# A hybrid decoder layer on one core: decay rows in HBM by chunk, and a third slot for the gating tile

## The chip, the core and the metric

The kernel runs on one core of a Trainium2 chip. The core has five engines that run side by side, each through its own instructions in order: TensorE (PE, matrix products), VectorE (DVE), ScalarE (ACT), GpSimd (POOL), and SyncE (SP), which here only issues transfers. Transfers run on 16 DMA engines between HBM and the on-chip memory of 128 partitions. The metric is the device time of one execution in microseconds (us).

## What is computed

One layer of a decoder over 1024 tokens (and 16 learned ones ahead): a projection of the normed input feeds three branches (linear attention, sliding-window attention, and a state-space branch, SSD), which are gated, merged, projected and followed by an MLP. The change concerns SSD alone. Cut to that:

```
a_cs = jnp.cumsum(dtc * A, axis=2)                          # decay sums inside a chunk of 128 tokens
xdt = xc * dtc[..., None]
seg = a_cs[:, :, :, None] - a_cs[:, :, None, :]
Lmat = jnp.exp(jnp.where(causal[:, :, None, None], seg, -jnp.inf))
CB = jnp.einsum('bnlgd,bnsgd->bnlsg', Cc, Bc)
y_diag = jnp.einsum('bnlsgh,bnsghp->bnlghp', CB[..., None] * Lmat, xdt)
...
y_off = jnp.einsum('bnlgd,bnghpd->bnlghp', Cc, S_prev) * jnp.exp(a_cs)[..., None]
y = y_diag + y_off + D_skip.astype(f32).reshape(SSD_GROUPS, SSD_HPG)[:, :, None] * xc
y = y.reshape(bsz, L, SSD_DINNER) * jax.nn.silu(z.astype(f32))
y = y * lax.rsqrt(jnp.mean(y * y, axis=-1, keepdims=True) + EPS)    # per group of 512 channels
```

There are 32 heads of 64 channels, in four groups of eight heads, and eight chunks of 128 tokens.

## The kernel before

Everything runs in float32; large products are made of three passes over a high and a low part of each operand. A first phase holds the normed input on chip and makes all projections; a second does the branch projections, merging and the MLP.

Early in the first phase the cumulated decays of all 32 heads stand in the tile `stk`, one head per partition. L753 stores them to HBM as `acs_d`, 32 rows of 1024 tokens. Behind it on SP come `dec_d` (L754), its load `decb` (L758) and weight loads (`w_raw`, L160).

The function `ssd(g)` (L570) does one group. It makes the convolved inputs, then a loop over eight chunks `c` (L651), with two slots each for most tiles. A chunk goes like this:

- SP loads `ab` (L654): the chunk's 128 decays of each of the group's eight heads, the same for all 128 partitions (512 KB on chip), and `zt` (L656), the gate, 256 KB.
- VectorE subtracts each partition's own decay (L658, eight instructions), ScalarE takes Exp (L660), VectorE multiplies by C·B (L661) and makes xd (L663).
- TensorE multiplies `ab` by xd, head by head (L666), then makes the part from the state (L672) and the state's update (L683).
- VectorE sums y (L677, L676, L678) and the new state (L686); GpSimd prepares some terms (L674, L681, L685).
- y is multiplied by `zt` (L688), squared and summed by ScalarE, which writes over `zt` (L690), scaled (L86, L88, L692), transposed by TensorE (L644) and stored (`y_out`, L641).

A slot of `ab` is free when L666 of the chunk two before has read it. A slot of `zt` is free when L690 of its chunk has ended. In between, TensorE gets products of other stages as fillers: the gates (`fill`, stores from L224) and the next group's z (`zfill`, L199 to L201, stored to `zd` by L213); their weights come through L160, and L143 and L144 split them into high and low parts (three slots for `w_raw`). A scheduler sets the order of each engine's instructions when the kernel is built, from the priorities in the code; the chip keeps that order.

Of the kernel before, what the change touches and what calls it, by code (L numbers as in the profile page):

```python
# [8 lines left out]
F32 = mybir.dt.float32  # L9
# [7 lines left out]
P = 128  # L17
D = 1024
KD = D // P
SEQ = 1024  # L20
NM = 16
T = NM + SEQ
NT = SEQ // P
# [21 lines left out]
def hybrid_layer_kernel(ctx, tc, x, meta_tokens, norm_mix, w_in, b_gate, gla_w_gate_up, gla_b_gate_up,  # L45
# [3 lines left out]
    nc = tc.nc  # L49
# [10 lines left out]
    dram = ctx.enter_context(tc.tile_pool(name="dram", bufs=1, space=DRAM))  # L60
# [46 lines left out]
    ossd = [dram.tile([512, SEQ], F32, name=f"ossd{g}") for g in range(4)]  # L107
    gated = [dram.tile([P, SEQ], F32, name=f"gate{i}") for i in range(24)]
    zd = [dram.tile([SEQ, 512], F32, name=f"zd{i}") for i in range(4)]
    acs_d = dram.tile([32, SEQ], F32, name="acs_d")  # L110
    dec_d = dram.tile([32, NT], F32, name="dec_d")
    x2_d = dram.tile([SEQ, D], F32, name="x2_d")
    hid_d = {(q, n): dram.tile([256, 512], F32, name=f"hid{q}_{n}")
# [65 lines left out]
    with p1:  # L179
# [390 lines left out]
        def ssd(g):  # L570
            CH = 512
# [78 lines left out]
            with tc.high_priority(offset=HPE):  # L650
                for c in range(NT):  # L651
                    cs = slice(NM + c * P, NM + (c + 1) * P)
                    ab = ep.tile([P, 8, P], F32, tag="ab", name="ab", bufs=2)
                    nc.sync.dma_start(ab, acs_d[8 * g:8 * g + 8, c * P:(c + 1) * P].partition_broadcast(P))  # L654
                    zt = ep.tile([P, CH], F32, tag="zt", name="zt", bufs=2)
                    nc.sync.dma_start(zt, zd[g][c * P:(c + 1) * P, :])  # L656
                    for h in range(8):
                        nc.vector.tensor_scalar(ab[:, h, :], ab[:, h, :], tms[:, c, 32 + 8 * g + h:33 + 8 * g + h], 0.0,  # L658
                                                op0=sub, op1=amin)
                    nc.scalar.activation(ab, ab, AF.Exp)  # L660
                    nc.vector.tensor_tensor(ab, ab, up(cb[:, c, :], 1, [P, 8, P]), mult)  # L661
                    xd = ep.tile([P, CH], F32, tag="xd", name="xd", bufs=2)
                    nc.vector.tensor_tensor(r3(xd), r3(xT[:, c, :]), tcol(c, 0), mult)  # L663
                    psD = bank(bk, "y", 3)
                    for h in range(8):
                        mm = nc.tensor.matmul(psD[:, h * 64:(h + 1) * 64], lhsT=ab[:, h, :],  # L666
                                              rhs=xd[:, h * 64:(h + 1) * 64], start=True, stop=True)
                    if c:
                        with tc.issue_after(mm.ins):
                            y_out(c - 1, yn)  # L670
                    psY = bank(bk, "y", 3)
                    nc.tensor.matmul(psY, lhsT=CF[:, cs], rhs=S, start=True, stop=True)  # L672
                    y = ep.tile([P, CH], F32, tag="y", name="y", bufs=2)
                    nc.gpsimd.tensor_tensor(r3(y), r3(xT[:, c, :]), up(db[:, 8 * g:8 * g + 8], 2, s3), mult)  # L674
                    t2 = ep.tile([P, CH], F32, tag="t2", name="t2", bufs=1)
                    nc.vector.tensor_tensor(r3(t2), r3(psY), tcol(c, 2), mult)  # L676
                    nc.vector.tensor_tensor(y, y, psD, add)  # L677
                    nc.vector.tensor_tensor(y, y, t2, add)  # L678
                    if c < NT - 1:
                        xe = ep.tile([P, CH], F32, tag="xe", name="xe", bufs=2)  # L680
                        nc.gpsimd.tensor_tensor(r3(xe), r3(xT[:, c, :]), tcol(c, 3), mult)  # L681
                        psS = bank(bk, "y", 3)
                        nc.tensor.matmul(psS, lhsT=BT[:, c, :], rhs=xe, start=True, stop=True)  # L683
                        S2 = ep.tile([P, CH], F32, tag="S", name="S", bufs=2)
                        nc.gpsimd.tensor_tensor(r3(S2), r3(S), up(decb[:, 8 * g:8 * g + 8, c], 2, s3), mult)  # L685
                        nc.vector.tensor_tensor(S2, S2, psS, add)  # L686
                        S = S2
                    nc.vector.tensor_tensor(y, y, zt, mult)  # L688
                    ss = sm.tile([P, 1], F32, tag="ss", name="yss")
                    nc.scalar.activation(zt, y, AF.Square, accum_out=ss)  # L690
                    rs = rstd_of(ss, CH, "yrs")
                    nc.scalar.activation(y, y, AF.Copy, scale=rs)  # L692
                    yn = y
                y_out(NT - 1, yn)
# [4 lines left out]
        with tc.tile_pool(name="dtp", bufs=1, reuse_waits="tile") as dp, bank_pool("bdt") as bk:  # L699
            def loads(raw, i):  # L700
                rv = raw.rearrange("p (k c) -> p k c", k=KD // 2)
                ks = slice(i * (KD // 2), (i + 1) * (KD // 2))
                nc.gpsimd.memset(rv[:, :, 16:32], 0.0)
                nc.sync.dma_start(rv[:, :, 0:16], w_in_v[:, ks, GLR:GLR + 16])
                nc.sync.dma_start(rv[:, :, 32:64], w_in_v[:, ks, MDT:MDT + 32])
            w = w_split(loads, 64)
            dtb = dp.tile([64, 1], F32, name="dtb")
            nc.scalar.dma_start(dtb[32:64, :], ssd_dt_bias[0].unsqueeze(1))
            an = dp.tile([64, 1], F32, name="an")
            nc.scalar.dma_start(an[32:64, :], ssd_A_log[0].unsqueeze(1))  # L710
            r = slice(32, 64)
            nc.scalar.activation(an[r], an[r], AF.Exp)
            nc.vector.tensor_scalar(an[r], an[r], -1.0, None, op0=mult)
            e = dp.tile([64, T], F32, name="dte")
            dt = dp.tile([64, T], F32, name="dt")

            def ev(ps, c0, n):
                nc.scalar.copy(lrT[:, c0:c0 + n], ps[0:16])
                nc.scalar.activation(e[r, c0:c0 + n], ps[r], AF.Abs, bias=dtb[r])
                nc.vector.tensor_scalar(dt[r, c0:c0 + n], ps[r], dtb[r], 0.0, op0=add, op1=amax)  # L720
            fm(w, 0, 64, PIECES, ev)
            wv_ = dp.tile([64, T], F32, name="dtw")
            ln = dp.tile([64, T], F32, name="dtl")
            nc.scalar.activation(e[r], e[r], AF.Exp, scale=-1.0)
            nc.vector.tensor_scalar(wv_[r], e[r], 1.0, None, op0=add)
            nc.scalar.activation(ln[r], wv_[r], AF.Ln)
            nc.vector.tensor_tensor(dt[r], dt[r], ln[r], add)
            nc.vector.tensor_scalar(ln[r], wv_[r], -1.0, None, op0=add)
            nc.vector.tensor_tensor(e[r], e[r], ln[r], sub)
            nc.vector.reciprocal(wv_[r], wv_[r])  # L730
            nc.vector.tensor_tensor(e[r], e[r], wv_[r], mult)
            nc.vector.tensor_tensor(dt[r], dt[r], e[r], add)
            stk = dp.tile([P, T], F32, name="stk")
            nc.vector.tensor_scalar(ln[r], dt[r], an[r], None, op0=mult)
            rst = dp.tile([64, T], F32, name="rst")
            nc.gpsimd.memset(rst[r], 1.0)
            nc.gpsimd.memset(rst[r, 0:1], 0.0)
            nc.gpsimd.memset(rst[r, NM:].rearrange("p (c t) -> p c t", t=P)[:, :, 0:1], 0.0)
            nc.vector.tensor_tensor_scan(out=stk[r], data0=rst[r], data1=ln[r], initial=0.0, op0=mult, op1=add)
            nc.scalar.copy(stk[0:32], dt[r])  # L740
            nc.scalar.activation(stk[64:96], stk[r], AF.Exp)
            sr = stk[r, NM:].rearrange("p (c t) -> p c t", t=P)
            nc.vector.tensor_tensor(wv_[r, NM:].rearrange("p (c t) -> p c t", t=P),
                                    sr[:, :, P - 1:P].broadcast_to([32, NT, P]), sr, sub)
            nc.vector.tensor_scalar(wv_[r, 0:NM], stk[r, 0:NM], stk[r, NM - 1:NM], -1.0, op0=sub, op1=mult)
            nc.scalar.activation(wv_[r], wv_[r], AF.Exp)
            nc.vector.tensor_tensor(stk[96:128], dt[r], wv_[r], mult)
            for t in range(NT + 1):
                ps = bank(bk, "tr", 4)
                c0, n = (NM + t * P, P) if t < NT else (0, NM)  # L750
                nc.tensor.transpose(out=ps[:n, :P], in_=stk[:, c0:c0 + n], identity=ident)
                nc.vector.tensor_copy(tms[:n, t, :], ps[:n, :P])
            nc.sync.dma_start(acs_d, stk[r, NM:])  # L753
            nc.sync.dma_start(dec_d.unsqueeze(2), stk[64:96, NM:].rearrange("p (c t) -> p c t", t=P)[:, :, P - 1:P])  # L754
        zfill(1000)
        fill(FD)
# [23 lines left out]
    with ExitStack() as p2:  # L780
# [68 lines left out]
        for b in range(2):  # L849
            for k in range(KD):  # L850
                t = hl_tile()
# [293 lines left out]
        for i in range(2):  # L1145
            t = hl_tile().bitcast(F32)
# [71 lines left out]
        for q in range(NQ):  # L1218
# [28 lines left out]
            c = four()  # L1247
# [44 lines left out]
```

## Time and profile before

| | us |
|---|---|
| median of 3 runs (2694.1 to 2702.11) | 2696.54 |
| the profiled execution | 2697.15 |
| its span, first to last instruction | 2695.5 |
| TensorE busy | 2612.5 (97%) |
| VectorE busy | 1502.5 (56%) |
| ScalarE busy | 1096.4 (41%) |
| GpSimd busy | 513.9 (19%) |

The mean granted clock of TensorE over the span is 0.983 of full speed. The four chunk loops of SSD run at about 940 to 1035, 1122 to 1217, 1327 to 1415 and 1505 to 1590 us of the span; the stretches between them make the next group's inputs. In a row of the timeline the time in brackets is how long the engine had stood idle before, with what released it; a busy TensorE isn't TensorE at its peak, since matrix products overlap.

### The profile page before, as it was taken

How to read it: one execution, taken by the hardware profiler on the slowest of the kernel's cores; microseconds unless marked ns; L12 is line 12 of the kernel's file. 1: busy time of each engine (PE TensorE's matmuls, PEld its weight loads, DVE VectorE, ACT ScalarE, POOL GpSimd, SP SyncE). 2: the span in 40 equal slices, each digit the busy share in tenths (PEclk: the TensorE clock that was granted, in tenths of full speed). 3: DMA queues.
4: the chain of work that ended last, by engine and by line, in shares of the span. 5: the costliest groups of instructions: out<-in, count | busy, mean ns of one | idle time of the engine just before them, and what ended most of it. 6: DMA issues, size and time to landing. Idle time of an engine off the chain costs nothing.

```text
span 2695.5 us, 36835 instructions
## 1 busy us (share of the span) xinstructions
PE 2612.5 (97%) x14373; PEld 2245.8 (83%) x14373; DVE 1502.5 (56%) x2577; ACT 1096.4 (41%) x1930; POOL 513.9 (19%) x402
## 2 busy tenths in 40 slices
PE   8999999999999989989989999999999999999998
PEld 7998988888888979869879778888898888878887
DVE  5333323256664674563665664254437878777777
ACT  6423423246664454353364343233216222333334
POOL 1000000002221030130120210222200433353223
PEclk9999999999999989989999999999999999999999
DMA  4211112212223143252252365343234644574442
GB/s 143 64 46 49 48 48 62 80 50 72 68 65 100 48 109 95 59 121 87 57 137 65 84 213 172 102 157 102 87 132 145 202 158 149 188 273 142 150 149 79
DMA packets 253747, 293.54 MB, mean 109 GB/s; under 512 B 16014, under 2 KB 184260, under 8 KB 253572
## 3 DMA queue, kind: packets, MB, share of 16 engines
q1 hardware_dynamic: 199876, 223.48, 27.8%
q10 hardware_dynamic: 52736, 64.56, 6.8%
q0 software_dynamic: 960, 3.15, 0.4%
q8 instruction: 113, 1.85, 0.3%
q14 instruction: 62, 0.51, 0.1%
HBM read 213.93 MB, written 77.20 MB: 108 GB/s over the span
## 4 chain that ended last, share of the span: by engine, by line
PE 83%; DMA 8%; DVE 4%; ACT 3%; issue 2%; POOL 0%; SPq 0%; ACTq 0%; DVEq 0%; POOLq 0%
PE pp_ps L798 9%; PE acc_ps L171 9%; PE acc_ps L172 9%; PE acc_ps L173 8%; DMA ab<-acs_d 6%; PE pp_ps L801 4%; PE pp_ps L1204 4%; PE pp_ps L1205 4%; PE pp_ps L1202 3%; PE pp_ps L954 3%; PE pp_ps L957 3%; PE pp_ps L956 3%; PE acc_ps L199 3%; PE acc_ps L201 3%; PE acc_ps L200 3%
## 5 line engine op out<-in xcount | busy, mean ns | idle before, releaser
L171 PE MATMUL acc_ps<-hh,w_hi 128*128 128x512 f32 (+6 forms) x1320 | 473.0, 358 | 2.4 <-ACT rt L365 1.7
L172 PE MATMUL acc_ps<-hl,w_hi 128*128 128x512 f32 (+6 forms) x1320 | 473.5, 359 | 0.0
L173 PE MATMUL acc_ps<-hh,w_lo 128*128 128x512 f32 (+6 forms) x1320 | 472.4, 358 | 0.0
L199 PE MATMUL acc_ps<-w_hi,hh 128*128 128x256 f32 x1056 | 305.0, 289 | 4.2 <-ACT zst L212 4.1
L201 PE MATMUL acc_ps<-w_hi,hl 128*128 128x256 f32 x1056 | 307.0, 292 | 0.0
L200 PE MATMUL acc_ps<-w_lo,hh 128*128 128x256 f32 x1056 | 306.7, 291 | 0.0
L171 PEld LDWEIGHTS acc_ps<-hh,w_hi 128*128 128x128 f32 (+1 forms) x1320 | 247.5, 188 | 32.7 <-issue 3.7
L144 DVE TENSOR_TENSOR w_lo<-w_raw,w_hi 128x1024 fp32r<-128x1024 f32 (+1 forms) x124 | 156.9, 1267 | 204.4 <-ACT w_hi L143 201.1
L173 PEld LDWEIGHTS acc_ps<-hh,w_lo 128*128 128x128 f32 (+1 forms) x1320 | 247.7, 188 | 26.7 <-issue 2.7
L172 PEld LDWEIGHTS acc_ps<-hl,w_hi 128*128 128x128 f32 (+1 forms) x1320 | 247.4, 187 | 26.8 <-issue 2.4
L143 ACT CAST w_hi<-w_raw 128x1024 fp32r<-128x1024 f32 (+1 forms) x124 | 128.4, 1036 | 206.9 <-PE acc_ps L172 86.7
L199 PEld LDWEIGHTS acc_ps<-w_hi,hh 128*128 128x128 f32 x1056 | 198.7, 188 | 12.3 <-issue 5.9
L201 PEld LDWEIGHTS acc_ps<-w_hi,hl 128*128 128x128 f32 x1056 | 198.6, 188 | 11.7 <-issue 11.0
L200 PEld LDWEIGHTS acc_ps<-w_lo,hh 128*128 128x128 f32 x1056 | 198.6, 188 | 6.3 <-issue 4.9
L798 PE MATMUL pp_ps<-o,w_hi 128*128 128x512 f32 x512 | 201.5, 398 | 1.1 <-ACT gst L223 1.1
L801 PE MATMUL pp_ps<-o,w_hi 128*128 128x512 f32 x512 | 200.5, 392 | 0.0
L1204 PE MATMUL pp_ps<-w_lo,o 128*128 128x512 f32 x448 | 178.5, 399 | 3.7 <-DVE w_lo L1192 3.7
L1205 PE MATMUL pp_ps<-w_hi,o 128*128 128x512 f32 x448 | 178.2, 398 | 0.0
L1202 PE MATMUL pp_ps<-w_hi,o 128*128 128x512 f32 x448 | 176.1, 397 | 1.2 <-ACT w_hi L1191 1.2
L954 PE MATMUL pp_ps<-o,w_hi 128*128 128x512 f32 x448 | 176.1, 396 | 1.1 <-ACT o L165 0.8
L956 PE MATMUL pp_ps<-o,w_hi 128*128 128x512 f32 x448 | 177.1, 395 | 0.0
L957 PE MATMUL pp_ps<-o,w_lo 128*128 128x512 f32 x448 | 176.3, 395 | 0.0
(326 smaller groups left out, 5150.5 us busy)
## 6 DMA issues: line engine op xcount, KB each, us to landing
w_raw<-in_w_in_dram SPq DMA_DIRECT2D x80, 512.0 KB, 3.8
ab<-acs_d SPq DMA_DIRECT2D x32, 512.0 KB, 8.9
g<-gate SPq DMA_DIRECT2D x64, 256.0 KB, 3.6
w_raw<-in_w_mlp_in_dram SPq DMA_DIRECT2D x32, 512.0 KB, 3.6
hid_t<-mt ACTq DMA_DIRECT2D x64, 256.0 KB, 2.3
raw<-hid_t SPq DMA_DIRECT2D x32, 512.0 KB, 4.0
gate<-gst ACTq DMA_DIRECT2D x48, 256.0 KB, 2.5
hid_x<-hid ACTq DMA_DIRECT2D x48, 256.0 KB, 3.2
```

Source lines behind the costliest of these rows:

```text
L171: nc.tensor.matmul(ps, lhsT=lh, rhs=rh, start=(i == 0), stop=False)
L172: nc.tensor.matmul(ps, lhsT=lh, rhs=rl, start=False, stop=False)
L173: nc.tensor.matmul(ps, lhsT=ll, rhs=rh, start=False, stop=(i == n - 1))
L199: nc.tensor.matmul(o, lhsT=h_h, rhs=whi[:, k, off:off + width], start=(k == 0), stop=False)
L200: nc.tensor.matmul(o, lhsT=h_h, rhs=wlo[:, k, off:off + width], start=False, stop=False)
L201: nc.tensor.matmul(o, lhsT=h_l, rhs=whi[:, k, off:off + width], start=False, stop=(k == KD - 1))
L798: nc.tensor.matmul(ps[b], lhsT=lh, rhs=xs[b][:, 0, :], start=(st and k == 0), stop=(sp_ and k == n - 1))
L801: nc.tensor.matmul(ps[b], lhsT=lh, rhs=xs[b][:, 1, :], start=False, stop=False)
L956: nc.tensor.matmul(ps, lhsT=h[:, kk, :], rhs=x[:, 1, :], start=False, stop=False, skip_group_check=True)
L957: nc.tensor.matmul(ps, lhsT=l[:, kk, :], rhs=x[:, 0, :], start=False, stop=(last and kk == 3), skip_group_check=True)
L1204: nc.tensor.matmul(ps[t], lhsT=xh[:, ts], rhs=wl, start=False, stop=False, skip_group_check=True)
L1205: nc.tensor.matmul(ps[t], lhsT=xl[:, ts], rhs=wh, start=False, stop=(last and kk == 3), skip_group_check=True)
```

## The change

`acs_d` becomes four arrays, one for each group, with a chunk's eight heads side by side: 8 x 128 floats, 4 KB in one piece. The load of `ab` reads this piece once for each partition, where it read eight pieces of 512 B, 4 KB apart. The one store of 32 x 1024 becomes four, each from eight partitions. And `zt` gets a third slot.

```
-    acs_d = dram.tile([32, SEQ], F32, name="acs_d")
+    acs_d = [dram.tile([NT, 8, P], F32, name=f"acs_d{g}") for g in range(4)]
...
-                    nc.sync.dma_start(ab, acs_d[8 * g:8 * g + 8, c * P:(c + 1) * P].partition_broadcast(P))
-                    zt = ep.tile([P, CH], F32, tag="zt", name="zt", bufs=2)
+                    nc.sync.dma_start(ab.rearrange("p h t -> p (h t)"), acs_d[g][c].rearrange("h t -> (h t)").partition_broadcast(P))
+                    zt = ep.tile([P, CH], F32, tag="zt", name="zt", bufs=3)
...
-            nc.sync.dma_start(acs_d, stk[r, NM:])
+            for g in range(4):
+                nc.sync.dma_start(acs_d[g].rearrange("c h t -> h c t"),
+                                  stk[32 + 8 * g:40 + 8 * g, NM:].rearrange("h (c t) -> h c t", t=P))
```

The instructions of TensorE, VectorE, ScalarE and GpSimd stand in the same order as before (lines behind the store are two higher). Only SP's queue differs.

First place: SP at the start of the second group's chunk loop. `zd_125` is that group's gate, `acs_d_129` its decays; weights (`w_raw`) stand between. Before:

```order
L654 DMA ab<-acs_d 128x8x128
L656 DMA zt<-zd_125 128x512 x2
L160 DMA w_raw<-in_w_in_dram 128x4x128 x2
L160 DMA w_raw<-in_w_in_dram 128x4x256 x7
L654 DMA ab<-acs_d 128x8x128
L656 DMA zt<-zd_125 128x512
L654 DMA ab<-acs_d 128x8x128
L656 DMA zt<-zd_125 128x512
L654 DMA ab<-acs_d 128x8x128
L656 DMA zt<-zd_125 128x512
```

and now:

```order
L656 DMA zt<-zd_125 128x512
L654 DMA ab<-acs_d_129 128x1024
L656 DMA zt<-zd_125 128x512 x2
L160 DMA w_raw<-in_w_in_dram 128x4x128 x2
L160 DMA w_raw<-in_w_in_dram 128x4x256 x7
L654 DMA ab<-acs_d_129 128x1024
L656 DMA zt<-zd_125 128x512
L654 DMA ab<-acs_d_129 128x1024
L656 DMA zt<-zd_125 128x512
L654 DMA ab<-acs_d_129 128x1024
```

Ahead of the nine weight loads there are now three `zt` loads of the group instead of two; behind them `ab` and `zt` still take turns, with each `zt` that of one chunk later than before.

Second place: SP at the end of the second group's loop, where the third group's first loads begin (`zd_126`, `acs_d_130`). Before:

```order
L654 DMA ab<-acs_d 128x8x128
L160 DMA w_raw<-in_w_in_dram 128x4x256
L654 DMA ab<-acs_d 128x8x128
L656 DMA zt<-zd_125 128x512
L654 DMA ab<-acs_d 128x8x128
L656 DMA zt<-zd_125 128x512
L654 DMA ab<-acs_d 128x8x128
L160 DMA w_raw<-in_w_in_dram 128x4x256
L160 DMA w_raw<-in_w_in_dram 128x4x128 x2
L656 DMA zt<-zd_126 128x512 x2
```

and now:

```order
L654 DMA ab<-acs_d_129 128x1024
L160 DMA w_raw<-in_w_in_dram 128x4x256
L654 DMA ab<-acs_d_129 128x1024
L656 DMA zt<-zd_125 128x512
L654 DMA ab<-acs_d_130 128x1024 x2
L160 DMA w_raw<-in_w_in_dram 128x4x256
L160 DMA w_raw<-in_w_in_dram 128x4x128 x2
L656 DMA zt<-zd_126 128x512 x3
```

The last `zt` of the second group no longer stands between the third group's first two `ab` loads, and the third group loads three `zt` in a row.

## Rows read from the trace of the kernel before

**Rows 1.** Busy time in the four chunk loops, with granted clock

```profile
core 0: us, PE busy (x) PEld busy (x) DVE busy (x) ACT busy (x) POOL busy (x), PEclk, DMA share, GB/s
940.00:1035.00 95.00, 83.34 (x546) 71.19 (x545) 61.45 (x132) 51.75 (x73) 28.58 (x26) 0.89 0.50 125
1122.00:1217.00 95.00, 79.28 (x426) 63.57 (x424) 55.06 (x126) 41.53 (x60) 28.23 (x25) 0.86 0.46 109
...
1327.00:1415.00 88.00, 73.92 (x489) 62.37 (x488) 59.27 (x127) 50.78 (x71) 24.70 (x25) 0.94 0.51 123
1505.00:1590.00 85.00, 76.70 (x356) 59.03 (x354) 53.51 (x111) 28.92 (x48) 28.11 (x25) 0.90 0.40 110
```

**Rows 2.** The same view, 5 us of the second loop, behind an idle stretch

```profile
1152.00:1157.00 5.00, 5.00 (x19) 3.97 (x18) 2.10 (x3) 1.66 (x3) 1.37 (x1) 0.50 0.60 103
```

**Rows 3.** Line L654, who waited (us, times), and its landing

```profile
  DVE ab L658: 98.6, 27
...
DMA to landing us min/median/max: 7.5/8.9/10.2
```

**Rows 4.** SP's issues in the second loop, in order of time

```profile
1125.61 0.37 SPq L654 DMA_DIRECT2D ab<-acs_d  x1
1137.30 0.34 SPq L656 DMA_DIRECT2D zt<-zd  x1
1137.73 0.39 SPq L654 DMA_DIRECT2D ab<-acs_d  x1
```

**Rows 5.** ScalarE in the second loop, in order of time

```profile
1137.09 0.18 ACT L690 ACTIVATION_READ_ACCUMULATOR zt<-y 128x1 f32 x1
```

**Rows 6.** TensorE in the second loop, in order of time

```profile
1131.15 1.89 PE L666 MATMUL ps_y<-xd,ab 128*128 128x64 f32 x16
...
1150.33 0.69 PE L666 MATMUL ps_y<-xd,ab 128*128 128x64 f32 x2 [3.26 <-DVE y L677]
```

**Rows 7.** VectorE in the second loop, in order of time

```profile
1133.91 1.66 DVE L658 TENSOR_SCALAR ab<-ab,tms 128x128 f32<-128x128 f32 x8 [4.89 <-DMA ab<-acs_d]
...
1145.56 1.66 DVE L658 TENSOR_SCALAR ab<-ab,tms 128x128 f32<-128x128 f32 x8 [4.58 <-DMA ab<-acs_d]
...
1150.19 0.68 DVE L663 TENSOR_TENSOR xd<-xT,tms 128x512 f32<-128x512 f32 x1
```

**Rows 8.** Stretches as in rows 1, one us with the `ab` load in flight

```profile
1129.00:1130.00 1.00, 1.00 (x6) 0.77 (x6) 0.03 (x1) 0.00 (x0) 0.94 (x1) 1.00 0.39 87
```

**Rows 9.** The load of final_norm: its issue, and two us of its flight

```profile
L1236 SPq DMA_DIRECT2D o<-in_final_norm_dram x1: 340/340/340, 2620.0 to 2620.0; - x1
...
2621.00:2622.00 1.00, 1.00 (x6) 0.82 (x5) 1.00 (x1) 1.00 (x2) 1.00 (x1) 1.00 0.88 340
2622.00:2623.00 1.00, 1.00 (x6) 0.82 (x5) 1.00 (x1) 0.53 (x1) 0.09 (x1) 1.00 0.47 172
```

**Rows 10.** SP's issues behind the second loop, in order of time

```profile
1230.19 1.02 SPq L656 DMA_DIRECT2D zt<-zd  x2
1246.44 75.78 SPq L160 DMA_DIRECT2D w_raw<-in_w_in_dram  x9
```

**Rows 11.** SP's issues around the store of the decays

```profile
73.64 0.34 SPq L753 DMA_DIRECT2D acs_d<-stk  x1
```

**Rows 12.** Stretches as in rows 1, 10 us behind that store

```profile
80.00:90.00 10.00, 10.00 (x81) 8.80 (x80) 3.62 (x7) 3.69 (x7) 0.00 (x0) 1.00 0.59 143
```

**Rows 13.** VectorE in the third loop, in order of time

```profile
1364.78 0.29 DVE L658 TENSOR_SCALAR ab<-ab,tms 128x128 f32<-128x128 f32 x1 [0.92 <-DMA ab<-acs_d]
...
1374.55 2.41 DVE L658 TENSOR_SCALAR ab<-ab,tms 128x128 f32<-128x128 f32 x8 [0.18 <-DMA ab<-acs_d]
```

**Rows 14.** TensorE in the third loop, in order of time

```profile
1373.77 2.46 PE L666 MATMUL ps_y<-xd,ab 128*128 128x64 f32 x16 [1.76 <-DVE ms L86]
```

**Rows 15.** Issues of transfers: line, tile, count, KB each, us to landing

```profile
w_raw<-in_w_in_dram SPq DMA_DIRECT2D x36, 256.0 KB, 3.5
```

## The prediction

> **What bounds the kernel now.** I read the stages first (busy time of each engine in chosen stretches), then who waits for the `ab` load, then the queue of SP and the order of time on VectorE, ScalarE and TensorE inside one loop. Over the whole span TensorE is busy 2612.5 of 2695.5 us, so only 83 us of its idle time can be won, plus what a lowered clock costs. Both sit mostly in four short stretches: the chunk loops of the four SSD groups [rows 1]. There TensorE is busy 83.34 of 95, 79.28 of 95, 73.92 of 88 and 76.70 of 85 us, at a granted clock of 0.89, 0.86, 0.94 and 0.90. Busy time times the granted clock is the work that TensorE has there at its full clock, an estimate from the rows: 83.34 x 0.89 = 74.2, then 68.2, 69.5 and 69.0, in sum 280.9 of 363 us. So **82 us is the ceiling** of what these loops can give: about 50 us of idle time, the rest clock. In the slices behind an idle stretch the granted clock is 0.50 with TensorE busy all the time [rows 2], the lower of its two levels (1.2 of 2.4 GHz).
>
> What causes the idle time is the `ab` load of L654. VectorE stood still 98.6 us in 27 waits for it, and a load takes 7.5 to 10.2 us from issue to landing, 8.9 in the middle [rows 3]. VectorE takes its work in order, so behind the waiting L658 also stand the sums of the chunk before (L677, L676, L686) and xd (L663), for which TensorE waits.
>
> Only one `ab` load is ever on its way in the second loop, although there are two slots. SP issues it at 1137.73, right behind the `zt` load at 1137.30 [rows 4]. That `zt` waits for a slot, which L690 on ScalarE frees at 1137.27 (1137.09 + 0.18) [rows 5]. The slot of `ab` itself was free at 1133.04, when L666 of the chunk before ended (1131.15 + 1.89) [rows 6]. L690 in turn comes 3.4 us after VectorE began L658 at 1133.91, that is after the landing of the `ab` issued at 1125.61 [rows 4, 7]. So **a lap is landing time plus 3.4 us**: L658, Exp, L690, SP's `zt`, the next `ab`, its flight. 8.2 + 3.4 = 11.6 us, and the rows say 1145.56 - 1133.91 = 11.65 [rows 7]. TensorE needs 68.2 / 8 = 8.5 us a chunk there.
>
> **The change, part by part.**
>
> *The loads.* Each of the 32 `ab` loads has the same 512 KB, but as 128 runs of 4 KB in place of 1024 runs of 512 B. In flight, the old form keeps the 16 DMA engines busy at a share of 0.39 and moves 87 GB/s [rows 8]. The nearest row for the new form is the load of final_norm (L1236): also a broadcast of one 4 KB line of HBM to 128 partitions, 512 KB, issued at 2620.0; 340 + 172 = 512 of its 524 kB move in the two microseconds from 2621 to 2623 [rows 9]. So it is through some 3.0 us after its issue, without other traffic; inside the loops a `zt` load of 256 KB is issued 0.43 us ahead [rows 4], so I take **3.5 us** as landing time. The bounds are 3.0 (that row) and 8.9 (no change); I choose the first because source, destination and run length are the same.
>
> *Where that puts the laps.* Landing plus 3.4 us falls from 11.65 to 6.9 us, below the 8.5 us that TensorE needs; up to a landing time of 5.1 us TensorE stays the later one. One lap worked through, in the second loop: `ab` issued at 1125.61 lands at 1129.1; L690 ends 3.4 us later at 1132.5; the next `ab` waits then for its slot and goes at 1133.1 (1133.04 above), landing at 1136.6 rather than 1145.56. L663 of that chunk ended 5.3 us after the landing (1150.19 + 0.68 - 1145.56) [rows 7], so it would be done near 1142, or 1.3 us behind L666 of the chunk before if that is later. TensorE reaches that chunk's L666 at 1147.07 (1150.33 - 3.26) [rows 6]. The wait of 3.26 us is gone with some 4 us to spare, and with it the slow clock behind it.
>
> *The third slot of `zt`.* By the order of SP the third slot only brings each `zt` one place forward. Counting chunks from 0: ahead of `ab` 3 stood `zt` 2, now `zt` 3. Before, `zt` 2 waited for L690 of chunk 0 (two slots); now `zt` 3 waits for L690 of chunk 0 (three slots). It is the same wait at the same place of the queue. I cost the slot at nothing, gain or loss: what frees SP earlier is the shorter landing. At a group's end one more `zt` stands ahead of nine weight loads; it is ready about 3 us behind its sister at 1230.19, and the first of the nine goes only at 1246.44 [rows 10]. Without that cover it would cost those 3 us, three times.
>
> *The stores.* One store of 128 KB becomes four of 32 KB, so SP issues three more: 3 x 0.34 = 1.0 us [rows 11]. Behind them stand dec_d, decb and weight loads; TensorE is busy 10.00 of 10 us there [rows 12], so nothing, or 1.0 us if that cover fails. The first reader of the rows comes at 850 us. TensorE, VectorE, ScalarE and GpSimd keep their order, row by row.
>
> *What is late next.* With `ab` on time VectorE is next: busy 61.45, 55.06, 59.27 and 53.51 us against 74.2, 68.2, 69.5 and 69.0 of TensorE [rows 1], 78 to 85 percent. It isn't the bound on average, but in single laps it is. In the third loop, from 1364.78 to 1374.55, VectorE waited for `ab` 0.18 us only, so it worked 9.6 us for one chunk; TensorE's need there is 69.5 / 8 = 8.7, and it waited 1.76 us before its L666 [rows 13, 14]. Such waits stay. I count two such laps in the first and the third loop, where fillers bring most work to VectorE, and one in each of the others: 6 x 1.76 = 10.6 us. For the heads and tails of the loops (y of the last chunk, with no chunk behind it) I add 1 us each, 4 us. That is about 15 us of the 82 that stay.
>
> *Sum.* 82 - 15 = 67 us. Against the profiled execution's own 2697.15 us (span 2695.5 and 1.65 around it): 2697.15 - 67 = **2630 us**. The median of the runs, 2696.54, is 0.6 us below the profiled one, which changes nothing here.
>
> **The rivals.**
>
> *VectorE and ScalarE take over (2656 us).* If at 78 to 85 percent share the in-order chain of L658, Exp, L661, L663 makes TensorE wait in most laps, half of the ceiling stays: 41 us won. For it: the 9.6 us lap above. Against it: the lap worked through has 4 us to spare.
>
> *Run length isn't what makes the load slow (2697 us).* Were the flight set by 512 KB read 128 times from one place, landing would stay at 8.9, the lap at landing plus 3.4, and since the third `zt` slot leaves the same wait in place, the time stays within 1 us. For it: weight loads of 256 KB in 512 runs of 512 B land in 3.5 us [rows 15], so short runs alone can't be the reason. Against it: the final_norm row [rows 9]. The Trainium skill's "DMA: Bandwidth & Descriptors" (Specifications) states that 512 B is the least transfer for line rate. By that rule the old runs are at line rate already and this rival's 2697 would be the time; the old load's 87 GB/s speaks against the rule, for this many runs at least.
>
> *Many readers of one 4 KB line are slower than of eight rows (2733 us).* All 16 DMA engines now read the same 4 KB; before, the reads were spread over eight rows 4 KB apart. If they hinder each other, landing grows, and it decides from 8.9 us on: each us above that lengthens a lap by one. At 10.2, the longest landing of now [rows 3], that is +1.3 us in seven laps of each of four loops: 28 x 1.3 = 36 us. The final_norm row speaks against it, too.
>
> **How the numbers follow.** Forecast (2630, own range 2613 to 2645): 0.74. VectorE takes over (2645 to 2668): 0.14. Landing unchanged (2697): 0.08. Slower (2733): 0.04. About 0.3 percent, 8 us, is what a measurement of this kernel can tell from no change. The best end is 2697.15 - 82 - 2 = 2613: all of the ceiling, and 2 us since the clock's rows have two digits (0.005 of 363 us). For 8 in 10 the range takes in the forecast's own part and half of the first rival's: 2613 to 2657. Faster: 0.74 + 0.14 = 0.88; same 0.08; slower 0.04.
>
> **What the profile of the changed kernel would show.** Landing of `ab` near 3.5 us; above 5.1 the step of the load is wrong. Waits of L658 for `ab` below 15 us in sum rather than 98.6. In the loops a granted clock of 0.97 or more and TensorE idle for 15 us in sum; the loops some 78, 72, 73 and 73 us long. SP's `ab` issues directly behind the end of an L666 rather than behind an L690. The stretches between the loops as long as now. If landing is short and the loops aren't, VectorE's lap was mis-sized; if idle time moves to the stretches between the loops, weight loads were hidden behind the `ab` waits.

## The result

The changed kernel takes 2634.61 us (median of 4 runs, 2633.53 to 2636.43), the kernel before 2697.57 beside it (4 runs, 2694.1 to 2702.11). The ratio is 0.9766, with a 95% interval of 0.9749 to 0.9783: 63 us less, where 67 were forecast. The profiled execution took 2633.53 us, its span is 2631.8 us, and the mean granted clock is 0.997.

The page of the changed kernel, busy time by engine and the chain that ended last:

```profile
PE 2576.6 (98%) x14373; PEld 2220.3 (84%) x14373; DVE 1518.9 (58%) x2577; ACT 1096.3 (42%) x1930; POOL 516.7 (20%) x402
...
PE 87%; DVE 6%; ACT 3%; issue 2%; DMA 1%; POOL 0%; ACTq 0%; SPq 0%; DVEq 0%; POOLq 0%
```

Transfers hold 1 percent of the chain, where they held 8 percent of it before. What is left beside TensorE is mostly VectorE. Line L654 of the changed kernel, who waited for the load (us, times), and its time from issue to landing:

```profile
  DVE ab L658: 14.3, 8
...
DMA to landing us min/median/max: 3.7/3.9/5.7
```

Against [rows 3], landing fell from 8.9 to 3.9 us and the waits from 98.6 to 14.3 us. The four chunk loops of the changed kernel, with columns as in [rows 1]; each window runs from its loop's first L666 to the end of its last transpose L644:

```profile
943.67:1018.59 74.92, 67.27 (x471) 57.62 (x470) 62.43 (x126) 49.69 (x69) 26.58 (x25) 0.98 0.46 140
1110.83:1182.33 71.50, 65.31 (x416) 54.33 (x415) 60.19 (x126) 41.49 (x60) 29.70 (x25) 1.00 0.43 136
1291.20:1365.26 74.06, 67.03 (x471) 57.12 (x470) 62.16 (x126) 49.69 (x69) 26.58 (x25) 0.98 0.48 142
1457.37:1527.32 69.95, 68.29 (x348) 52.41 (x346) 57.52 (x111) 29.06 (x48) 28.99 (x25) 1.00 0.40 128
```

Between the same two instructions, the loops of the kernel before took 86.2, 93.6, 85.8 and 84.2 us (945.26 to 1031.44, 1123.69 to 1217.24, 1328.10 to 1413.88 and 1506.04 to 1590.26). So the loops lost 11, 22, 12 and 14 us, 59.3 of the 63.7 us by which the span fell. TensorE's idle time in them is 22.5 us (290.4 - 267.9), and the granted clock is 0.98 to 1.00 where it was 0.86 to 0.94. Of the other 4.4 us, 2.0 lie behind the second loop, where the clock was 0.98 and is now 1.00, 1.6 ahead of the first loop and 0.8 behind the fourth. The fourth loop came down to nearly what TensorE needs: it is idle for 1.7 us there, and for 7.7, 6.2 and 7.0 us in the other three. VectorE is busy for 82 to 84 percent of each of the four.

### The profile page after: what moved, and what is told of

Same layout as the page of the kernel before. It is cut to its first block, busy times and chain, and to the rows that moved or that the text cites. A ratio compares the mean times of both kernels' runs of the same rounds, so it can differ in the third digit from the quotient of the medians.

```text
span 2631.8 us, 36869 instructions
## 1 busy us (share of the span) xinstructions
PE 2576.6 (98%) x14373; PEld 2220.3 (84%) x14373; DVE 1518.9 (58%) x2577; ACT 1096.3 (42%) x1930; POOL 516.7 (20%) x402
## 2 busy tenths in 40 slices
DMA packets 225315, 293.54 MB, mean 112 GB/s; under 512 B 16030, under 2 KB 151764, under 8 KB 225140
## 4 chain that ended last, share of the span: by engine, by line
PE 87%; DVE 6%; ACT 3%; issue 2%; DMA 1%; POOL 0%; ACTq 0%; SPq 0%; DVEq 0%; POOLq 0%
PE pp_ps L800 9%; PE acc_ps L171 9%; PE acc_ps L172 9%; PE acc_ps L173 9%; PE pp_ps L803 5%; PE pp_ps L1206 4%; PE pp_ps L1207 4%; PE pp_ps L1204 4%; PE pp_ps L956 4%; PE pp_ps L959 4%; PE pp_ps L958 4%; PE acc_ps L199 3%; PE acc_ps L201 3%; PE acc_ps L200 3%; DVE ab L658 1%
## 5 line engine op out<-in xcount | busy, mean ns | idle before, releaser
L201 PEld LDWEIGHTS acc_ps<-w_hi,hl 128*128 128x128 f32 x1056 | 196.0, 186 | 11.1 <-issue 10.4
```

Source lines behind the costliest of these rows:

```text
L201: nc.tensor.matmul(o, lhsT=h_l, rhs=whi[:, k, off:off + width], start=False, stop=(k == KD - 1))
```

## The experiments

Two questions were open. Which part of the edit makes the load land earlier, since it changes three things at once (the length of a run, the distance of the eight rows from one another, the slots of `zt`)? And what holds the laps of the first and third loop now, where most idle time is left? Ratios are to the kernel before, run beside each experiment on the same chip.

### The two halves of the edit

The layout alone, with two `zt` slots:

```
-                    zt = ep.tile([P, CH], F32, tag="zt", name="zt", bufs=3)
+                    zt = ep.tile([P, CH], F32, tag="zt", name="zt", bufs=2)
```

> The new layout with two slots for zt. My theory: the third slot leaves the same wait ahead of each ab load on SP (L690 of the same chunk), so the layout alone gives all of the gain: ab lands in 3.9 us as with the whole change, time 2635 us, within 4 us of it. Rival (the slot is worth something once the landing is short, since a zt load no longer waits for the chunk before): SP's ab issues come later behind zt, L658's waits grow from 14 us to 30 or more and the time is 2645 to 2660.

Measured: 2633.76 us, ratio 0.9747 (0.9731 to 0.9764); landing 3.6 us in the middle, waits of L658 11.5 us.

The third slot alone, in the old layout:

```
-                    zt = ep.tile([P, CH], F32, tag="zt", name="zt", bufs=2)
+                    zt = ep.tile([P, CH], F32, tag="zt", name="zt", bufs=3)
```

> The old layout (runs of 512 B, 4 KB apart) with three slots for zt. My theory: ab lands in 8.9 us as before, the lap in the second loop stays at landing plus 3.4, some 11.6 us, and the time is 2697 us, within 4 us of before. Rival (a third slot takes the wait for L690 away from ahead of the ab load, so that a lap falls to half of landing plus 7.5, 8.2 us): the second and fourth loop win 25 to 35 us in sum, time 2662 to 2672.

Measured: 2706.44 us, ratio 1.0018 (1.0009 to 1.0028). Line L654 of this kernel:

```profile
  DVE ab L658: 103.7, 25
...
DMA to landing us min/median/max: 8.0/9.3/10.3
```

The layout is the whole gain. The third slot wins nothing, as costed from SP's order: each `zt` moves one place forward and meets the same wait. Alone it makes the kernel 4.7 us slower than the kernel before beside it, a little more than the 4 us that were allowed for; why isn't shown.

### Is it the length of a run?

The changed kernel's arrays, but with every 512 B followed by 512 B of nothing, so that a load is again 1024 runs of 512 B, now 1 KB apart:

```
-    acs_d = [dram.tile([NT, 8, P], F32, name=f"acs_d{g}") for g in range(4)]
+    acs_d = [dram.tile([NT, 8, 2 * P], F32, name=f"acs_d{g}") for g in range(4)]
...
+                    nc.sync.dma_start(ab, acs_d[g][c][:, 0:P].partition_broadcast(P))
```

> The new layout with each head's 512 B at a pitch of 1 KB instead of side by side, so an ab load has 1024 runs of 512 B again, out of one stretch of 8 KB; all else as in the changed kernel. Theory A (the number of runs sets the flight): landing 8.9 us, time 2697 us within 5. Rival B (it was the pitch of 4 KB between the eight rows): landing near 3.9 us, time 2635 us. Something between would say that both count.

Measured: 2634.66 us, ratio 0.975 (0.9736 to 0.9765). From its page, the packets:

```profile
DMA packets 253987, 293.54 MB, mean 111 GB/s; under 512 B 16030, under 2 KB 184532, under 8 KB 253812
```

Its line L654:

```profile
  DVE ab L658: 14.4, 11
...
DMA to landing us min/median/max: 3.7/3.9/6.0
```

The packets are back near the number of the kernel before (253747; the changed kernel has 225315), and landing stays at 3.9 us. **So it is not the length of a run.** The Trainium skill's "DMA: Bandwidth & Descriptors" (Specifications) states that a transfer of 512 B is enough for line rate; this run agrees, with 3.9 us for runs of 512 B and of 4 KB alike.

A form between, runs of 1 KB that start 1.5 KB apart (`dram.tile([NT, 4, 3 * P], ...)`):

> As the run of 512 B pieces, but two heads side by side: 512 runs of 1 KB (a pitch of 1.5 KB). Theory A, on a line between 3.9 us at 128 runs and 8.9 at 1024 (5.6 ns a run): landing 6.0 us. Then a lap of landing plus 3.4 is 9.4 us against TensorE's 8.5 in the second and fourth loop, 0.9 us in each of ten laps, and some waits in the other loops: time 2644 to 2655 us. Rival B (pitch): 3.9 us and 2635. Four more stores on SP early on, 1.4 us, are hidden in all of these.

Measured: 2636.64 us, ratio 0.9755 (0.9741 to 0.977); waits of L658 15.1 us. In its second loop two loads for which VectorE stood waiting were issued at 1115.05 and 1123.99, and L658 began at 1118.80 and 1127.89, 3.8 and 3.9 us later. It says the same: theory A had 6.0 us.

### Is it the distance between the eight rows?

The kernel before with each row of `acs_d` made 512 B longer, 4608 B from row to row instead of 4096. The load reads the same 1024 runs, one store fills the array, there are two slots, and every engine has its instructions in the same order:

```
-    acs_d = dram.tile([32, SEQ], F32, name="acs_d")
+    acs_d = dram.tile([32, SEQ + P], F32, name="acs_d")
...
-            nc.sync.dma_start(acs_d, stk[r, NM:])
+            nc.sync.dma_start(acs_d[:, 0:SEQ], stk[r, NM:])
```

> The kernel before with one thing changed: its 32 decay rows lie 4608 B apart in HBM instead of 4096; runs of 512 B, one array, two zt slots, the same order on every engine. Theory B (the pitch of 4 KB between the eight rows that a load reads makes it slow): landing near 3.9 us, time 2635 us within 4. Rival C (what helps is one array for each group, or rows of a chunk close together, within 8 KB): landing stays at 8.9, time 2700.

Measured: 2635.25 us (2633.59 to 2637.05), ratio 0.9749 (0.9733 to 0.9765). Line L654 of this kernel:

```profile
  DVE ab L658: 11.6, 11
...
DMA to landing us min/median/max: 3.6/4.1/6.1
```

A pad of two lines of code gives what the whole change gives. The reverse, the changed kernel's four arrays and three slots with a chunk's eight rows set 4096 B apart again (`dram.tile([NT, 8, 8 * P], ...)`):

> The changed kernel's four arrays by group and three zt slots, but each head's 512 B at a pitch of 4096 B: chunk by chunk eight rows 4 KB apart, as before. Theory B: landing 8.9 to 9.3 us again and 2700 to 2706 us. Rival C (arrays by group are what helps): 3.9 us, 2635.

Measured: 2712.84 us, ratio 1.0031 (1.0018 to 1.0044). Its line L654:

```profile
  DVE ab L658: 109.5, 24
...
DMA to landing us min/median/max: 6.3/9.4/11.1
```

The slow landing is back, as theory B has it; the time lies 7 us above the range that it gave.

Rows 2048 B apart (`dram.tile([NT, 8, 4 * P], ...)`):

> As the run before this one with a pitch of 2048 B. If only rows 4 KB apart hinder each other: landing 3.9 us and 2635 us. If it is a matter of how many of the eight rows fall on the same place, and half of them still do: landing between, 5.5 to 6.5 us; then a lap of landing plus 3.4 is 8.9 to 9.9 us against TensorE's 8.5, time 2640 to 2660.

Measured: 2647.93 us, ratio 0.9793 (0.9778 to 0.9807); landing 6.0 us, waits of L658 33.6 us. And the kernel before with a pad of only 128 B (`SEQ + 32`):

> The kernel before, with each of the 32 rows 128 B longer (4224 B from row to row rather than 4096); nothing else, the order of every engine is the same. Theory P1 (only rows that start at exactly the same place of a 4 KB period hinder each other): any pad will do, landing 3.9 to 4.3 us, 2635 us. Theory P2 (the places are coarser than 128 B: eight rows of 512 B shifted by 128 B each still cover 1408 of the 4096 B of a period and lie over one another): landing between that of the 2 KB pitch and of the 4 KB pitch, 6 to 8.5 us, 2650 to 2690 us. I hold P2 the likelier, since the 2 KB pitch, with two places, gave 6.0 us.

Measured: 2649.54 us, ratio 0.9797 (0.9781 to 0.9814). Its line L654:

```profile
  DVE ab L658: 39.8, 22
...
DMA to landing us min/median/max: 5.2/5.9/7.7
```

That is just under what the second theory gave, and far from the 3.9 to 4.3 us of the first. All forms in a table:

| distance of the eight rows | run | landing, us | waits of L658, us | ratio |
|---|---|---|---|---|
| 4096 B (the kernel before with a third slot) | 512 B | 9.3 | 103.7 | 1.0018 |
| 4096 B (four arrays) | 512 B | 9.4 | 109.5 | 1.0031 |
| 2048 B | 512 B | 6.0 | 33.6 | 0.9793 |
| 4224 B | 512 B | 5.9 | 39.8 | 0.9797 |
| 4608 B | 512 B | 4.1 | 11.6 | 0.9749 |
| 1536 B | 1024 B | 3.8 and 3.9 (two loads) | 15.1 | 0.9755 |
| 1024 B | 512 B | 3.9 | 14.4 | 0.975 |
| none between (the change) | 4096 B | 3.9 | 14.3 | 0.9766 |

Landing follows how the rows lie in steps of 4096 B: all at the same place 9.4, at two places 6.0, shifted by a quarter of their own length 5.9, at four places or shifted by their whole length about 4. What in HBM stands behind it isn't shown by any run here. The distance alone isn't slow: the loads of the output weights, 512 KB as one run of 1 KB from each of 512 rows that lie 4 KB apart, land in 3.5 us, by the transfers of the kernel before (line, tile, count, KB each, us to landing):

```profile
w_raw<-in_w_out_dram SPq DMA_DIRECT2D x8, 512.0 KB, 3.5
```

They read every row once; `ab` reads eight rows 128 times each. That this repetition is the other half of the cause is argued from the pair, not tried. The Trainium skill's "DMA: Bandwidth & Descriptors" (Latency and other measured facts) tells of row distances at powers of two from 512 KiB up: the rate falls with the distance, to about half at 4 MiB, where a pad of 4 KiB restores it and one of 192 B doesn't, and the cause given is called an inference. Here something like it shows at 4 KB, for rows that are read over and over, and a pad of 512 B restores it; whether the cause is the same no run here shows.

### The queue, with the load left slow

By the prediction a second `ab` load can't start since it stands behind a `zt` load on SP. The kernel before with `zt` on ScalarE's queue:

```
-                    nc.sync.dma_start(zt, zd[g][c * P:(c + 1) * P, :])
+                    nc.scalar.dma_start(zt, zd[g][c * P:(c + 1) * P, :])
```

> The kernel before (rows 4 KB apart, ab lands in 8.9 us) with the zt load issued by ScalarE's queue instead of SP's, so that no ab load stands behind a zt. My theory of the lap: an ab load then goes as soon as its slot is free, a lap of the second and fourth loop falls from landing plus 3.4 (11.6 to 12.4 us) to half of landing plus 7.5, 8.2 us, where TensorE's 8.5 take over; the first and third loop, where ab already goes right behind L666, stay. Win 20 to 32 us, time 2668 to 2680. Rival (the wait behind zt isn't what sets the lap): within 6 us of before.

Measured: 2698.69 us, ratio 0.9979 (0.9969 to 0.999); landing 8.9, waits of L658 92.2 us. The expectation of 2668 to 2680 us missed. VectorE in its second loop, in order of time:

```profile
1138.80 1.66 DVE L658 TENSOR_SCALAR ab<-ab,tms 128x128 f32<-128x128 f32 x8 [5.00 <-DMA ab<-acs_d]
...
1146.28 1.57 DVE L658 TENSOR_SCALAR ab<-ab,tms 128x128 f32<-128x128 f32 x6 [0.41 <-DMA ab<-acs_d]
...
1172.71 1.66 DVE L658 TENSOR_SCALAR ab<-ab,tms 128x128 f32<-128x128 f32 x8 [5.27 <-DMA ab<-acs_d]
```

SP of the same kernel, ahead of the last of these waits:

```profile
1161.81 0.37 SPq L160 DMA_DIRECT2D w_raw<-in_w_in_dram  x1
1162.27 6.07 SPq L654 DMA_DIRECT2D ab<-acs_d  x2
```

The lap that was 11.65 us [rows 7] is 7.48 here (1146.28 - 1138.80), so the reading of the queue was right for that lap. But two chunks later the load stands behind a weight load at 1161.81, though its slot had been free since 1156.28, when an L666 ended, and VectorE waits 5.27 us again. Taking one wait out of the queue is worth 0.2 percent while a load takes 8.9 us.

### What holds the first and third loop

In the third loop of the changed kernel VectorE doesn't wait for `ab` over two laps, and yet TensorE waits. VectorE there, in order of time:

```profile
1304.32 2.47 DVE L658 TENSOR_SCALAR ab<-ab,tms 128x128 f32<-128x128 f32 x8
...
1308.04 1.53 DVE L663 TENSOR_TENSOR xd<-xT,tms 128x512 f32<-128x512 f32 x1
1309.49 2.06 DVE L661 TENSOR_TENSOR ab<-ab,cb 128x1024 f32<-128x1024 f32 x1
...
1312.73 2.48 DVE L658 TENSOR_SCALAR ab<-ab,tms 128x128 f32<-128x128 f32 x8
```

GpSimd in the same stretch:

```profile
1304.48 1.06 POOL L685 TENSOR_TENSOR S<-S,decb 128x512 f32<-128x512 f32 x1
1307.65 1.37 POOL L681 TENSOR_TENSOR xe<-xT,tms 128x512 f32<-128x512 f32 x1 [2.11 <-PE ps_y L683]
1308.98 1.49 POOL L674 TENSOR_TENSOR y<-xT,db 128x512 f32<-128x512 f32 x1
```

TensorE at the end of that lap:

```profile
1312.21 2.00 PE L666 MATMUL ps_y<-xd,ab 128*128 128x64 f32 x16 [1.32 <-DVE ms L86]
```

A lap of VectorE is 8.41 us (1312.73 - 1304.32). Each of the long instructions lies beside one of GpSimd: L658 takes 2.47 rather than the 1.66 of [rows 7], L663 1.53 rather than 0.68. To test it, the three multiplications of GpSimd (L674, L681, L685) go to VectorE:

```
-                    nc.gpsimd.tensor_tensor(r3(y), r3(xT[:, c, :]), up(db[:, 8 * g:8 * g + 8], 2, s3), mult)
+                    nc.vector.tensor_tensor(r3(y), r3(xT[:, c, :]), up(db[:, 8 * g:8 * g + 8], 2, s3), mult)
...
-                        nc.gpsimd.tensor_tensor(r3(xe), r3(xT[:, c, :]), tcol(c, 3), mult)
+                        nc.vector.tensor_tensor(r3(xe), r3(xT[:, c, :]), tcol(c, 3), mult)
...
-                        nc.gpsimd.tensor_tensor(r3(S2), r3(S), up(decb[:, 8 * g:8 * g + 8, c], 2, s3), mult)
+                        nc.vector.tensor_tensor(r3(S2), r3(S), up(decb[:, 8 * g:8 * g + 8, c], 2, s3), mult)
```

> The changed kernel, with the three 128x512 multiplications that GpSimd does for each chunk (y by D, xe, S by the decay) on VectorE; the scheduler moves some other instructions. Theory V (VectorE's instructions with all inputs in SBUF take up to 0.84 us longer while GpSimd works, and that holds the laps of the first and third loop): with GpSimd out of the way L658 of eight goes from 2.48 to 1.66, L661 from 2.06 to 1.22, L663 and L688 from 1.53 to 0.68 wherever they were stretched, some 2.5 us a chunk less, against 3 x 0.68 = 2.0 us more work: VectorE's laps of 8.4 to 9.0 us become 0.3 to 0.6 shorter, and the time is 2618 to 2634 us. Rival R (the stretch has another cause, such as transfers into SBUF): the long rows stay, 2.0 us are added to each lap, and the first and third loop grow by 10 to 16 us each: 2650 to 2665 us.

Measured: **2617.09 us** (2615.32 to 2618.14), ratio 0.9678 (0.9664 to 0.9693): faster than both kernels, and 1 us under the lower end of the theory. Groups of VectorE's instructions by form (busy us, mean ns of one, idle before), of the changed kernel:

```profile
L658 DVE TENSOR_SCALAR ab<-ab,tms 128x128 f32<-128x128 f32 x256 | 73.8, 354 | 14.3 <-DMA ab<-acs_d 14.3
...
L661 DVE TENSOR_TENSOR ab<-ab,cb 128x1024 f32<-128x1024 f32 x32 | 45.7, 1438 | 6.3 <-ACT ab L660 6.3
...
L663 DVE TENSOR_TENSOR xd<-xT,tms 128x512 f32<-128x512 f32 x32 | 28.5, 902 | 0.0
...
L686 DVE TENSOR_TENSOR S<-S,ps_y 128x512 f32<-128x512 f32 x28 | 18.9, 674 | 0.0
```

The same groups of this kernel:

```profile
L658 DVE TENSOR_SCALAR ab<-ab,tms 128x128 f32<-128x128 f32 x256 | 54.2, 286 | 18.7 <-DMA ab<-acs_d 18.7
...
L661 DVE TENSOR_TENSOR ab<-ab,cb 128x1024 f32<-128x1024 f32 x32 | 38.8, 1224 | 10.6 <-ACT ab L660 10.4
...
L663 DVE TENSOR_TENSOR xd<-xT,tms 128x512 f32<-128x512 f32 x32 | 22.0, 688 | 0.0
...
L686 DVE TENSOR_TENSOR S<-S,ps_y 128x512 f32<-128x512 f32 x28 | 19.1, 683 | 0.0
```

L661 falls from 1438 to 1224 ns, L663 from 902 to 688, and eight of L658 from 73.8 / 32 = 2.31 to 1.69 us. L686, one of whose inputs lies in PSUM, stays; so do L676 and L677 (680 and 677 before, 688 and 685 now), of which the same is true. VectorE took over 88 instructions of 0.69 us, 61 us of work. The five lines with all inputs in SBUF gave back 42 us of that by their groups (L658, L661 and L663 above, L688 from 28.8 to 22.1 and L678 from 24.6 to 22.1), and VectorE's busy time over the span rose by 3.5 us only (1518.9 to 1522.4). The Trainium skill's "SBUF — State Buffer" (Who interferes with whom) says that a VectorE instruction with two SBUF inputs, or in a two-port mode, shares a port with GpSimd, and that the one that starts later waits; these rows agree, L686 included. Whether L658, with one such input, runs in a two-port mode no row here shows.

The loops of this kernel can't be compared window by window, since the scheduler puts more of the fillers into them (521 matrix products in the second, where the changed kernel has 416). From the first L666 of the second loop to that of the third the work is nearly the same; the changed kernel first, columns as in [rows 1]:

```profile
1110.83:1291.20 180.37, 174.18 (x1178) 161.64 (x1177) 110.54 (x202) 81.45 (x129) 36.16 (x30) 1.00 0.33 99
```

This kernel:

```profile
1105.85:1278.88 173.03, 173.03 (x1186) 161.85 (x1185) 113.28 (x224) 85.03 (x131) 5.74 (x8) 1.00 0.34 104
```

This stretch is 7.3 us shorter, and TensorE has no idle time left in it, where it had 6.2 us. From the first loop to the second it is 6.5 us, from the third to the fourth 7.1. The same with the three multiplications left out:

```
-                    nc.gpsimd.tensor_tensor(r3(y), r3(xT[:, c, :]), up(db[:, 8 * g:8 * g + 8], 2, s3), mult)
-                    nc.vector.tensor_tensor(y, y, psD, add)
+                    nc.vector.tensor_tensor(y, xT[:, c, :], psD, add)
...
-                        nc.tensor.matmul(psS, lhsT=BT[:, c, :], rhs=xe, start=True, stop=True)
+                        nc.tensor.matmul(psS, lhsT=BT[:, c, :], rhs=xT[:, c, :], start=True, stop=True)
...
-                        nc.vector.tensor_tensor(S2, S2, psS, add)
+                        nc.vector.tensor_tensor(S2, S, psS, add)
```

> The changed kernel with the same three multiplications left out (y takes x without D, the state takes x without its weight and is not decayed), so that GpSimd has next to nothing to do in the loops and VectorE and TensorE have the same instructions; the scheduler orders many instructions anew. Theory V: L658, L661, L663 and L688 at 1.66, 1.22, 0.68 and 0.68 us, 2.5 us less in each lap of VectorE, so the first and the third loop come down to what TensorE needs; of the 16 us that they still lost against the ceiling 10 to 16 come back: 2618 to 2625 us. Rival R: the long rows stay and the time is that of the changed kernel within 4 us, 2630 to 2638 us.

Measured: 2611.98 us, ratio 0.9661 (0.9647 to 0.9676), some 6 us under the lower end of the theory; L661 takes 1223 ns and L663 686. With GpSimd out of the way only 5 us are left between doing this work on VectorE and not doing it. This kernel's loops hold about as many matrix products as those of the changed kernel (460, 406, 459 and 348 against 471, 416, 471 and 348), and TensorE's idle time in them fell from 22.5 to 6.7 us, so the gain doesn't need more fillers in the loops. But both kernels have some instructions in another order, and this one has fewer steps, too, so how much of the 17 us (2634.61 - 2617.09) is the port and how much the order isn't separated.

Last, the same move in the kernel before, where the load is still slow:

> The kernel before (old layout, 4096 B from row to row, two slots), with the three multiplications of each chunk on VectorE instead of GpSimd. Theory L (while an ab load takes 8.9 us, it sets the laps; in the second loop VectorE stood still 4.6 to 4.9 us of every lap of 11.65, so neither the 2.0 us of added work nor the 2.5 us saved shows): landing stays at 8.5 to 9.3 us, the waits of L658 at 85 to 110 us in sum, the time within 6 us of the kernel before. Rival A (the two changes add up): the 17 us that the same edit took off the changed kernel come off here, too, a ratio near 0.9935, some 2680 us beside a kernel before of 2697.

Measured: 2682.85 us, ratio 0.993 (0.9914 to 0.9947). My theory, that nothing would show, missed; the number is the rival's. But it came in another place. Landing, from line L654 of this kernel:

```profile
DMA to landing us min/median/max: 7.6/9.1/10.9
```

Landing is what it was. From the first L666 of its second loop to that of the third, columns as in [rows 1]:

```profile
1122.34:1313.48 191.14, 180.25 (x1186) 166.76 (x1185) 113.26 (x224) 84.42 (x131) 6.88 (x8) 0.96 0.36 94
```

The kernel before took 204.41 us for the same stretch (1123.69 to 1328.10), so 13.3 of the 18.9 us by which the span fell lie here, 3.2 between the first loop and the second, and 0.8 between the third and the fourth; in the changed kernel the same edit gave some 7 us in each. SP at the start of that second loop:

```profile
1124.27 0.37 SPq L654 DMA_DIRECT2D ab<-acs_d  x1
1131.47 0.37 SPq L654 DMA_DIRECT2D ab<-acs_d  x1
1136.01 0.33 SPq L656 DMA_DIRECT2D zt<-zd  x1
```

VectorE there:

```profile
1132.62 1.66 DVE L658 TENSOR_SCALAR ab<-ab,tms 128x128 f32<-128x128 f32 x8 [3.45 <-DMA ab<-acs_d]
...
1139.85 1.66 DVE L658 TENSOR_SCALAR ab<-ab,tms 128x128 f32<-128x128 f32 x8 [0.79 <-DMA ab<-acs_d]
```

The scheduler put two `ab` loads ahead of the two `zt`, so that the second goes out before the first has landed, where [rows 4] show one `zt` between them. This lap is 7.23 us (1139.85 - 1132.62) in place of 11.65, with L658 at 1.66 us in both kernels: an effect of order, not of a shorter VectorE. It is 4.4 of the 13.3 us; where the rest comes from isn't traced. That the two gains agree in size (17 and 19 us) is chance as far as these rows show, and a warning for the 17 us above.

## Why the prediction was right, point by point

**The place and the ceiling** held: 59.3 of the 63.7 us came out of the four loops, under the ceiling of 82.

**The landing time** was taken as 3.5 us; it measured 3.9, and 3.6 with two slots. The number was right and one of the three reasons given for it was not: "source, destination and run length are the same". Run length does nothing (3.9 us with 512 B). What the final_norm load has in common with the new form is that its reads don't go to eight rows 4 KB apart. By the reason given, the kernel with runs of 512 B 1 KB apart would have stayed at 2697 us; it took 2634.66. The edit was made for the length of a run and won because it removed the distance as well, and that part of the right forecast was luck. The prediction also took the old load's 87 GB/s to speak against the rule on 512 B; that step failed, since the rule stands and the 87 GB/s have another cause. The rival "run length isn't what makes the load slow" was right in its name and wrong in its time: it took for granted that nothing else in the layout changed.

**The lap** was to fall below TensorE's 8.5 us with `ab` issued as soon as its slot is free. In the second and fourth loop that step failed for most laps, and the time came out right by a narrow margin. SP in the second loop of the changed kernel, in order of time:

```profile
1121.26 0.34 SPq L656 DMA_DIRECT2D zt<-zd  x1
1121.69 0.38 SPq L654 DMA_DIRECT2D ab<-acs_d  x1
1129.88 0.32 SPq L656 DMA_DIRECT2D zt<-zd  x1
1130.36 0.32 SPq L654 DMA_DIRECT2D ab<-acs_d  x1
```

VectorE between these issues, where the load of 1121.69 has landed:

```profile
1125.46 2.64 DVE L658 TENSOR_SCALAR ab<-ab,tms 128x128 f32<-128x128 f32 x8 [0.52 <-DMA ab<-acs_d]
```

ScalarE, at the end of that chunk's gate:

```profile
1129.66 0.19 ACT L690 ACTIVATION_READ_ACCUMULATOR zt<-y 128x1 f32 x1
```

`ab` still goes right behind a `zt` that waited for L690 (1129.66 + 0.19 = 1129.85). Landing to the end of L690 is 4.39 us (1129.85 - 1125.46) and not 3.4: L658 takes 2.64 us in place of 1.66, beside GpSimd. The lap is 1130.36 - 1121.69 = 8.67 us, about what TensorE needs (8.5), and not the 6.9 of the prediction: in such a lap the margin of 1.6 us is gone. Of this loop's six `ab` issues three go right behind a `zt` and one behind a weight load; two, at 1112.76 and 1152.70, go right behind the end of an L666 (1112.72 and 1152.66), as forecast for all of them. Over the loop's eight chunks L666 came every 7.9 us (1110.83 to 1165.96).

**The third slot** at nothing: right for this change, by the two halves of the edit (2633.76 us without it, 2634.61 with it). **The stores** at nothing: right within what the runs can tell.

**What stays** was the mis-sized term: 15 us forecast, 25 measured (290.4 us of loops less 265.2 of work at full clock, busy time times the granted clock by the rows above). TensorE's waits over the whole span of the changed kernel (us, times, longest):

```profile
PE ps_tr L644 <- ACT y L692: 10.5, 12, 2.2
...
PE ps_y L666 <- DVE ms L86: 8.7, 7, 1.7
...
PE ps_y L666 <- DVE t L676: 1.7, 2, 0.9
```

The waits before L666 for VectorE, 8.7 + 1.7 = 10.4 us, are what was counted (10.6). Missing are the 10.5 us in 12 waits of the transpose L644 for y, of which the prediction had only 4 us, at heads and tails; the remaining 4 us are 3 of clock and some small waits. By the forecast lengths of 78, 72, 73 and 73 us against [rows 1], the loops were to lose 17, 23, 15 and 12 us; they lost 11, 22, 12 and 14, so 8 us of the 67 are missing, and they are missing in the first and third. The 4.4 us outside the loops, where the prediction had nothing, made up half of that: the stretch behind the second loop became 2.0 us shorter, the other two between the loops stayed as long as they were, as forecast. The sum is closer than its terms.

**The rival that VectorE takes over** was partly true: in the third loop VectorE set a lap of 8.4 us, and part of its time was stretched by GpSimd, which the prediction hadn't seen: the 9.6 us lap that it counted from [rows 13] has L658 at 2.41 us, not 1.66.

**The rival of many readers of one line** fell with the landing time: all partitions now read the same 4 KB, and no load of the changed kernel takes longer than 5.7 us.

## What to carry to other kernels

When a broadcast load reads a few rows over and over, look at the distance between the rows before the length of a run: rows 4096 B apart cost 5 us a load here (9.4 against 4.1), and a pad of 512 B per row removed it without touching anything else. Before such a price is put on one property of a layout, list every property that the edit changes. And where VectorE becomes dense, compare each of its instructions with the shortest one of the same form: those that are longer beside GpSimd point to work that may be cheaper on VectorE itself.

## What the runs showed of the hardware that was not expected

- 512 KB as 1024 runs of 512 B land in 3.9 us with the rows 1024 B apart, 4.1 at 4608 B, 5.9 at 4224 B, 6.0 at 2048 B and 9.4 at 4096 B.
- GpSimd's three multiplications of 512 columns cost VectorE a large part of what doing them itself costs: moving 61 us of work to it took 42 us off its lines with all inputs in SBUF, and its busy time rose by 3.5 us. Its lines with an input in PSUM didn't change (674 and 683 ns for L686).
